# A transformer layer on one core: the sums for the first feed-forward half made beside the values, its first block in seven products, and the values' residual rows added by DVE

## The chip, the cores and the metric

The kernel runs on one core of one Trainium2 chip. A core has a matrix engine (TensorE; the profile calls its matmuls PE and its weight loads PEld), a vector engine (DVE), a scalar engine (ACT), a general engine (POOL) and SyncE (SP), which here only issues transfers (DMA). Each engine works through its own instructions in the order in which they were placed; semaphores tie the engines together. The metric is device microseconds of one execution; lower is better. Before the change the median of 3 runs is 2623.56 us (2621.81 to 2627.48).

## The reference, cut to what matters

One layer of an encoder trunk on 2048 tokens of width 1024, all in 32-bit floats. The change touches the end of step 2 and the beginning of step 3.

```
h = h + rms_norm(y, g_mix_post)                 # after token mixing
u = rms_norm(h, g_x_pre);  m = rms_norm(mem, g_mem)
y = cross_attention(u, m, wq_x, wk_x, wv_x, wo_x)   # 4 heads, 256 memory tokens
h = h + rms_norm(y, g_x_post)
u = rms_norm(h, g_ffn_pre)
y = (silu(u @ w_gate) * (u @ w_up)) @ w_down    # inner width 2816
h = h + rms_norm(y, g_ffn_post)
```

## The kernel before, in words

Every 32-bit matrix is split into a high and a low part of a rounded type ("fp32r"), and a product takes three matmuls (high x high, high x low, low x high; `products`, lines 1009 to 1019). The later phases are written as a list of jobs (`jobs`, line 1277): out projection (mixing), cross-attention scores, cross-attention values, first feed-forward half (tokens 0 to 1023), second half (tokens 1024 to 2047), and the down projection in three passes. In scores and values the weights of the memory side are folded beforehand, so each is one matrix product.

A job multiplies a stationary side, streamed block by block (`streamed`, line 964, whose pieces are called S), with a resident side (called T). Both are cut in 2 x 2 quarters. A block of kind "p" makes the four quarters of its result with eight products of quarters (`eight`); a block of kind "s" makes them with seven (`seven`), for which S and T must also be given as sums and differences of quarters. The T's are numbered by keys: keys 1, 8, 2 and 3 are plain quarters; keys 5, 7, 6 and 4 (`CHAIN`) are differences and sums: 5 is the second column quarter less the first in the upper row, 7 the lower right less the upper right, 6 is 7 plus the upper left, 4 is the lower left less 6. In a block of kind "s" the products come in the order 1, 5, 6, 3, 7, 2, 4; in one of kind "p" two at a time for keys 1, 2, 8, 3. One product has 4 x 3 matmuls of 128x512 where `nk` is 4.

In the mixing, scores and values a block takes 256 tokens (two token tiles of 128) as S, against a weight as T. In the two feed-forward halves it is the other way: u, transposed and stored in `u_d`, is T (1024 tokens of it, quarters by token and by width), and 256 columns of `w_gate` or `w_up` are S. So the first half's T's are made from what the value blocks stored for token tiles 0 to 7 (value blocks 1 to 4 of 8).

`phases` (line 1098) is the planner. It numbers all steps (one product of a block of kind "s", or two of kind "p"), lists each T with the steps that use it, and gives it one of seven T buffers as soon as the last use of what lies there has passed, in the order of first use. A T is loaded in two halves, one per step (two per step in blocks of kind "p"), each into a row tile of 128x1024 (`row_tile`, line 1318; there are nine, shared with everything else of that size, and they are handed out in the order of the program). `resident` (line 893) then splits it with ACT (line 886) and DVE (line 889). For keys 5, 7, 6 and 4 there are two ways: a job with a sums tensor loads them ready-made, one load per half, and splits them two steps later, behind the step's own ACT and DVE work; a job without one (`None`, as the first feed-forward half has) loads the two quarters, keeps those of 7 and 6 for the next key, and adds or subtracts on DVE at line 915. The ready-made sums of the other jobs are computed beside an earlier job (`combined`, line 926, DVE at line 933) and stored.

What follows a block (`after`) is a generator: the planner advances it once per step of the next blocks (twice per step of kind "p"). In `value_block` (line 1440) it takes the mean squares of the two rows y, scales them (line 1459), adds the residual rows h1 by an accumulating transfer that POOL issues (`add`, line 1365), stores h2 through SP, takes mean squares again (line 1336, ACT), scales into two new row tiles u (line 1470), transposes u on PE (line 1252, back through ACT at 1253) and stores it to `u_d`. All other loads and stores are issued by SP (lines 75 and 78), one after another. `mixed_block` (line 1367) does the same for its own residual with plain loads and an addition on DVE (line 1386).

The instructions are traced in this order; a scheduling pass then places them on each engine by their data, their tiles and this order.

Of the kernel before, what the change touches and what calls it, by code (L numbers as in the profile page):

```python
# [11 lines left out]
F32 = mybir.dt.float32  # L12
# [3 lines left out]
ALU = mybir.AluOpType  # L16
AX = mybir.AxisListType

P = 128
# [5 lines left out]
KT = D // P  # L25
NFF = DFF // P
# [22 lines left out]
class Layer:  # L49
# [1011 lines left out]
    def eight(self, S, T, nk, out, addend, halves=False):  # L1061
# [34 lines left out]
        yield  # L1096

    def phases(self, jobs, first, prologue=None):

        steps = [(n, i, p) for n, job in enumerate(jobs) for i, b in enumerate(job[2])
                 for p in self.STEPS[b[0]]]
        takes = [c for job in jobs for b in job[2] for c in self.TAKES[b[0]]]
# [161 lines left out]
    def sums(self, name, src, nk, *tiles):  # L1266
# [7 lines left out]

        return dst, lambda: self.combined(get, nk, dst)

    def jobs(self):
        I = self.I

        def weights(src, r0, nk):  # L1280
            return lambda t, i, j, k0, n: self.load(
                t, src[r0 + (i * nk + k0) * P:r0 + (i * nk + k0 + n) * P, j * 512:(j + 1) * 512]
                .rearrange("(k p) d -> p k d", p=P))

        def ffn_u(b):
            return lambda t, i, j, k0, n: self.load(
                t, self.u_d[4 * i + k0:4 * i + k0 + n, :, b * TB + j * 512:b * TB + (j + 1) * 512]
                .rearrange("k p t -> p k t"))

        def kinds(blocks, n=0):  # L1290
            return [("p" if i < n or i == len(blocks) - 1 else "s",) + b for i, b in enumerate(blocks)]

        def sums(name, src, nk, other=None):
            return self.sums(name, src, nk, self.extra_tile, other or self.gain_tile)

        def in_turn(*what):
            return lambda: itertools.chain.from_iterable(w() for w in what)

        qk, vo = weights(self.qk_d, 0, 4), weights(self.vo_d, 0, 4)
        down = [(weights(I["w_down"], f0 * P, nk), f0, nk) for f0, nk in ((0, 3), (6, 4), (14, 4))]  # L1300
        qk_s, vo_s = sums("qk_s", qk, 4, self.row_tile), sums("vo_s", vo, 4)
        u_s = sums("u_s", ffn_u(1), 4)
        d_s = [sums(f"d_s{c}", src, nk) for c, (src, _, nk) in enumerate(down)]
        jobs = [(self.w_out, 4, kinds([self.mixed_block(n) for n in range(0, NT, 2)], 1), self.out_sums, {1: [qk_s[1]]}),
                (qk, 4, kinds([self.score_block(n) for n in range(0, NT, 2)]), qk_s[0], {1: [vo_s[1]]}),
                (vo, 4, kinds([self.value_block(n) for n in range(0, NT, 2)]), vo_s[0], {})]
        for b in range(NB):
            beside = {2: [in_turn(*(d[1] for d in d_s))]} if b else {4: [u_s[1]]}
            jobs.append((ffn_u(b), 4, kinds([blk for f in range(0, NFF, 2) for blk in self.hidden_blocks(b, f)], 1 - b),
                         u_s[0] if b else None, beside))  # L1310
        for c, (src, f0, nk) in enumerate(down):
            jobs.append((src, nk, kinds([self.down_block(c, f0, nk, n) for n in range(0, NT, 2)]), d_s[c][0], {}))
        k, s, o, f, a = jobs[-1][2][-1]
        jobs[-1][2][-1] = ("s", s, o, f, a)

        return jobs
# [122 lines left out]

    def value_block(self, n):  # L1440
        nc = self.nc
        y, ss = {}, []

        def out(i, j, a, b):
            if not y:
                ss.append(self.small("q_s", 4))
            if i not in y:
                y[i] = self.row_tile()
                if n == 0 and len(y) == 1:
                    self.g_x_post = self.gain(self.I["g_x_post"])  # L1450
                    self.g_ffn_pre = self.extra_tile()
                    self.load(self.g_ffn_pre, self.I["g_ffn_pre"][0:1, :].broadcast_to([P, D]))
            self.squared(y[i][:, j * 512:(j + 1) * 512], a, b, ss[0][:, 2 * i + j:2 * i + j + 1])

        def after():
            r = self.rstds(ss[0])
            s2 = self.small("q_s", 4)
            for i in range(2):
                nc.vector.scalar_tensor_tensor(y[i], y[i], r[:, i:i + 1], self.g_x_post, ALU.mult, ALU.mult)
                self.add(y[i], self.h1_d, n + i)  # L1460
                self.store(self.h2_d[(n + i) * P:(n + i + 1) * P, :], y[i])
                yield
            yield
            for i in range(2):
                self.mean_squares(y[i], i, s2)
                yield
            r = self.rstds(s2)
            u = [self.row_tile() for _ in range(2)]
            for i in range(2):
                nc.vector.scalar_tensor_tensor(u[i], y[i], r[:, i:i + 1], self.g_ffn_pre, ALU.mult, ALU.mult)  # L1470
                yield
            yield
            for i in range(2):
                self.store_transposed(self.u_d, n + i, self.transposed(u[i], u[i]))
                yield

        return self.tokens(self.pt_d, n), out, after, None

    def hidden_blocks(self, b, f):
# [130 lines left out]
```

## Time and profile before

| what | us |
|---|---|
| median of 3 runs | 2623.56 (2621.81 to 2627.48) |
| the profiled execution, whole | 2629.38 |
| its span in the profile | 2627.7 |
| PE busy | 2560.7 (97%) |
| DVE busy | 1732.1 (66%) |
| ACT busy | 1262.0 (48%) |
| POOL busy | 431.3 (16%) |
| mean granted clock of PE | 0.993 |

The profile is of one execution. Times in it count from the start of the span; an engine's idle time carries the name of what released it. Matmuls overlap, so the mean length of one is longer than the distance between two. A tile's buffer number is left out of its name: "row" is any of the nine row tiles, "sraw" a streamed block, "part" a copied partial result, "psm" a PSUM bank of the products, "pss" one of the transposes; "h_d" stands for h1 and h2.

### The profile page before, as it was taken

How to read it: one execution, taken by the hardware profiler on the slowest of the kernel's cores; microseconds unless marked ns; L12 is line 12 of the kernel's file. 1: busy time of each engine (PE TensorE's matmuls, PEld its weight loads, DVE VectorE, ACT ScalarE, POOL GpSimd, SP SyncE). 2: the span in 40 equal slices, each digit the busy share in tenths (PEclk: the TensorE clock that was granted, in tenths of full speed). 3: DMA queues.
4: the chain of work that ended last, by engine and by line, in shares of the span. 5: the costliest groups of instructions: out<-in, count | busy, mean ns of one | idle time of the engine just before them, and what ended most of it. 6: DMA issues, size and time to landing. Idle time of an engine off the chain costs nothing.

```text
span 2627.7 us, 34806 instructions
## 1 busy us (share of the span) xinstructions
PE 2560.7 (97%) x12329; PEld 2142.2 (82%) x12329; DVE 1732.1 (66%) x2725; ACT 1262.0 (48%) x2628; POOL 431.3 (16%) x627
## 2 busy tenths in 40 slices
PE   7999999999999999999989999999999999999998
PEld 6877888878988887888878888888888888888886
DVE  7675478877545778777676655566666556564656
ACT  5463366655545566565563333344333334453543
POOL 4231344331311332213310000000000000000022
PEclk9999999999999999999999999999999999999999
DMA  5445655675877886666884632353566434576888
GB/s 184 127 149 174 187 158 159 197 232 158 239 256 261 306 279 235 216 233 176 242 276 131 196 101 82 102 191 123 168 203 197 155 121 172 183 215 177 268 209 216
DMA packets 354158, 502.87 MB, mean 191 GB/s; under 512 B 20672, under 2 KB 237760, under 8 KB 353984
## 3 DMA queue, kind: packets, MB, share of 16 engines
q1 hardware_dynamic: 345632, 470.24, 55.0%
q0 software_dynamic: 8352, 30.41, 6.6%
q8 instruction: 97, 1.59, 0.3%
q14 instruction: 77, 0.63, 0.1%
HBM read 338.05 MB, written 162.53 MB: 191 GB/s over the span
## 4 chain that ended last, share of the span: by engine, by line
PE 81%; DMA 8%; DVE 4%; ACT 3%; issue 2%; POOL 1%; SPq 1%; DVEq 0%; POOLq 0%; ACTq 0%
PE psm L1017 23%; PE psm L1018 23%; PE psm L1019 23%; PE psg L158 2%; PE psg L157 2%; PE psg L156 2%; PE pss L1252 1%; DMA qd<-z_d 1%; DMA z<-in_w_out_dram 1%; DMA u_d<-row 1%; DMA qq<-z_d 1%; SPq L75 1%; DVE wlo L889 0%; DMA h_d<-row 0%; DMA row<-y_d 0%
## 5 line engine op out<-in xcount | busy, mean ns | idle before, releaser
L1017 PE MATMUL psm<-T,S 128*128 128x512 f32 x2699 | 1046.6, 392 | 18.7 <-ACT part L1032 9.4
L1018 PE MATMUL psm<-T,S 128*128 128x512 f32 x2699 | 1052.6, 391 | 0.7 <-DVE T L889 0.6
L1019 PE MATMUL psm<-T,S 128*128 128x512 f32 x2699 | 1042.7, 391 | 2.0 <-DVE S L889 2.0
L1017 PEld LDWEIGHTS psm<-T,S 128*128 128x128 f32 x2699 | 508.2, 188 | 129.7 <-ACT part L1032 10.6
L1019 PEld LDWEIGHTS psm<-T,S 128*128 128x128 f32 x2699 | 508.2, 188 | 108.3 <-DVE S L889 2.9
L1018 PEld LDWEIGHTS psm<-T,S 128*128 128x128 f32 x2699 | 508.3, 188 | 106.1 <-DVE T L889 2.1
L889 DVE TENSOR_TENSOR S<-sraw,S 128x512 fp32r<-128x512 f32 (+1 forms) x320 | 218.4, 689 | 215.9 <-ACT S L886 198.6
L886 ACT ACTIVATE S<-sum 128x512 fp32r<-128x512 f32 (+1 forms) x310 | 186.5, 620 | 345.0 <-PE psm L1019 257.9
L889 DVE TENSOR_TENSOR S<-sum,S 128x512 fp32r<-128x512 f32 (+1 forms) x368 | 246.8, 681 | 58.0 <-ACT S L886 34.6
L1032 ACT ACTIVATE part<-psm 128x512 f32<-128x512 f32 x270 | 159.9, 596 | 244.8 <-PE psm L1019 229.3
L886 ACT ACTIVATE S<-sraw 128x512 fp32r<-128x512 f32 (+1 forms) x273 | 168.0, 616 | 120.9 <-PE psm L1019 104.7
L1365 POOL DMA_DIRECT2D row<-y_d x28 | 25.8, 921 | 1124.4 <-DVE row L1541 1032.7
L889 DVE TENSOR_TENSOR T<-row,T 128x1024 fp32r<-128x1024 f32 (+1 forms) x122 | 143.7, 1191 | 66.5 <-ACT T L886 66.0
L156 PE MATMUL psg<-u,whi 128*128 128x512 f32 x352 | 141.5, 402 | 1.6 <-POOL whi L888 1.6
L158 PE MATMUL psg<-u,wlo 128*128 128x512 f32 x352 | 140.2, 398 | 0.9 <-DVE wlo L889 0.9
L157 PE MATMUL psg<-u,whi 128*128 128x512 f32 x352 | 140.3, 398 | 0.0
L886 ACT ACTIVATE T<-row 128x1024 fp32r<-128x1024 f32 x122 | 122.1, 1027 | 23.9 <-DVE row L915 7.8
L1336 ACT ACTIVATE junk<-row 128x512 f32<-128x512 f32 x160 | 99.9, 625 | 67.6 <-DVE row L1358 26.8
L888 POOL TENSOR_SCALAR S<-sum 128x512 fp32r<-128x512 f32 x58 | 48.3, 832 | 288.4 <-PE psm L1019 228.9
L1492 DVE TENSOR_TENSOR row<-psm,part 128x512 f32<-128x512 f32 x63 | 41.7, 688 | 59.5 <-PE psm L1019 59.4
L1501 DVE TENSOR_TENSOR part<-psm,part 128x512 f32<-128x512 f32 x60 | 39.8, 688 | 61.1 <-PE psm L1019 60.9
L156 PEld LDWEIGHTS psg<-u,whi 128*128 128x128 f32 x352 | 66.7, 189 | 14.7 <-POOL whi L888 2.1
(335 smaller groups left out, 3634.0 us busy)
## 6 DMA issues: line engine op xcount, KB each, us to landing
sraw<-in_w_gate_dram SPq DMA_DIRECT2D x44, 512.0 KB, 3.9
sraw<-in_w_up_dram SPq DMA_DIRECT2D x44, 512.0 KB, 4.0
hid_d<-row SPq DMA_DIRECT2D x44, 512.0 KB, 2.6
h_d<-row SPq DMA_DIRECT2D x32, 512.0 KB, 5.8
y_d<-row SPq DMA_DIRECT2D x32, 512.0 KB, 3.2
sraw<-hid_d SPq DMA_DIRECT2D x32, 512.0 KB, 5.1
row<-h_d POOLq DMA_DIRECT2D x30, 512.0 KB, 6.8
row<-u_d SPq DMA_DIRECT2D x30, 512.0 KB, 6.1
```

The lines of the kernel that those rows point to most:

```text
L156: nc.tensor.matmul(ps, ah, bh, start=(i == 0), stop=False)
L157: nc.tensor.matmul(ps, ah, bl, start=False, stop=False)
L158: nc.tensor.matmul(ps, al, bh, start=False, stop=(i == n - 1))
L886: self.nc.scalar.activation(hi, raw, AF.Copy)
L888: self.nc.gpsimd.tensor_scalar(hi, raw, 1.0, 1.0, ALU.mult, ALU.mult)
L889: self.nc.vector.tensor_tensor(lo, raw, f32(hi), ALU.subtract)
L1017: nc.tensor.matmul(ps, s[:, 0, k, :], t[:, 0, k, :], start=st, stop=False, **kw)
L1018: nc.tensor.matmul(ps, s[:, 0, k, :], t[:, 1, k, :], start=False, stop=False, **kw)
L1019: nc.tensor.matmul(ps, s[:, 1, k, :], t[:, 0, k, :], start=False, stop=sp, **kw)
L1032: nc.scalar.activation(t, ps, AF.Copy)
L1336: self.nc.scalar.activation(junk, a, AF.Square, scale=float(D) ** -0.5, accum_out=to)
L1492: nc.vector.tensor_tensor(d, a, c, ALU.add)
```

## The change

- `jobs`: a tensor `u0_s` holds ready-made sums for the first feed-forward half, and that job loads them (it had `None`). Its first block is of kind "s" (seven products) where it was "p" (eight). Its last block stays "p".
- `token_sums`: in the value blocks for token tiles 4 to 7, after u has been transposed and stored, the transposed u of token tile n - 4 is loaded back from `u_d` into a row tile o; eight half-row operations on DVE per block (four per token tile) turn u and o, in place, into the four sums for those 128 tokens, and four stores per token tile write them to `u0_s`.
- `value_block`: the residual rows x are loaded by SP into two row tiles when the block's first output is made, and DVE adds them; the accumulating transfers go. u overwrites y instead of taking new row tiles. The order of the `yield`s moves: there is one step less between the h2 stores and the mean squares, the step between the second scaling's factor and the scaling is new, and the one between the scaling and the transposes goes, so that the transposes are queued one step earlier.

```diff
+    def token_sums(self, a, o, n):
+        nc = self.nc
+        nc.vector.tensor_tensor(a[:, 4:8], a[:, 4:8], a[:, 0:4], ALU.subtract)
+        nc.vector.tensor_tensor(a[:, 0:4], a[:, 0:4], o[:, 0:4], ALU.subtract)
+        yield
+        nc.vector.tensor_tensor(o[:, 0:4], o[:, 0:4], a[:, 4:8], ALU.add)
+        nc.vector.tensor_tensor(o[:, 4:8], o[:, 4:8], o[:, 0:4], ALU.subtract)
+        for c, t in enumerate((a[:, 0:4], a[:, 4:8], o[:, 0:4], o[:, 4:8])):
+            self.store(self.u0_s[c].rearrange("p (k t) -> p k t", k=4)[:, :, n * P:(n + 1) * P], t)
+        yield
...
+        self.u0_s = self.tc.dram_tile([4, P, 4 * 512], F32, name="u0_s")
...
-            jobs.append((ffn_u(b), 4, kinds([blk for f in range(0, NFF, 2) for blk in self.hidden_blocks(b, f)], 1 - b),
-                         u_s[0] if b else None, beside))
+            jobs.append((ffn_u(b), 4, kinds([blk for f in range(0, NFF, 2) for blk in self.hidden_blocks(b, f)]),
+                         u_s[0] if b else self.u0_s, beside))
...
     def value_block(self, n):
-        y, ss = {}, []
+        y, x, ss, u, o = {}, [], [], {}, {}
         def out(i, j, a, b):
             if not y:
+                x.extend(self.rows_of(self.h1_d, n + r) for r in range(2))
...
             for i in range(2):
                 nc.vector.scalar_tensor_tensor(y[i], y[i], r[:, i:i + 1], self.g_x_post, ALU.mult, ALU.mult)
-                self.add(y[i], self.h1_d, n + i)
+                nc.vector.tensor_tensor(y[i], y[i], x[i], ALU.add)
                 self.store(self.h2_d[(n + i) * P:(n + i + 1) * P, :], y[i])
                 yield
-            yield
             for i in range(2):
                 self.mean_squares(y[i], i, s2)
                 yield
             r = self.rstds(s2)
-            u = [self.row_tile() for _ in range(2)]
-            for i in range(2):
-                nc.vector.scalar_tensor_tensor(u[i], y[i], r[:, i:i + 1], self.g_ffn_pre, ALU.mult, ALU.mult)
-                yield
             yield
             for i in range(2):
-                self.store_transposed(self.u_d, n + i, self.transposed(u[i], u[i]))
+                nc.vector.scalar_tensor_tensor(y[i], y[i], r[:, i:i + 1], self.g_ffn_pre, ALU.mult, ALU.mult)
                 yield
+            for i in range(2):
+                u[i] = self.transposed(y[i], y[i])
+                self.store_transposed(self.u_d, n + i, u[i])
+                if 4 <= n < 8:
+                    o[i] = self.row_tile().rearrange("p (k t) -> p k t", k=KT)
+                    self.load(o[i], self.u_d[:, :, (n - 4 + i) * P:(n - 3 + i) * P].rearrange("k p t -> p k t"))
+                yield
+            if o:
+                yield
+                for i in range(2):
+                    yield from self.token_sums(u[i], o[i], n - 4 + i)
```

## The prediction

> **What bounds the kernel now.** First the page: its busy times, then its chain.
>
> ```profile
> span 2627.7 us, 34806 instructions
> PE 2560.7 (97%) x12329; PEld 2142.2 (82%) x12329; DVE 1732.1 (66%) x2725; ACT 1262.0 (48%) x2628; POOL 431.3 (16%) x627
> PE 81%; DMA 8%; DVE 4%; ACT 3%; issue 2%; POOL 1%; SPq 1%; DVEq 0%; POOLq 0%; ACTq 0%
> ```
>
> PE holds the end, so only two things can shorten the run: fewer matmuls, or fewer holes between them. Second, the busy times by stretch around the edit (columns: stretch, its length, busy time and count of PE, PEld, DVE, ACT, POOL, granted clock, DMA share, GB/s).
>
> ```profile
> 1200.00:1250.00 50.00, 50.00 (x242) 41.83 (x241) 34.42 (x44) 28.90 (x68) 18.34 (x30) 1.00 0.72 197
> 1250.00:1300.00 50.00, 50.00 (x243) 41.70 (x242) 31.70 (x39) 27.43 (x63) 17.32 (x27) 1.00 0.85 222
> 1300.00:1350.00 50.00, 48.62 (x231) 40.34 (x230) 32.23 (x33) 30.19 (x60) 10.42 (x18) 1.00 0.99 295
> ...
> 1355.00:1375.00 20.00, 14.20 (x44) 9.79 (x43) 15.37 (x18) 12.18 (x19) 0.94 (x2) 0.74 0.80 288
> ...
> 2200.00:2300.00 100.00, 100.00 (x443) 82.80 (x442) 56.55 (x98) 40.99 (x78) 0.00 (x0) 1.00 0.49 169
> ```
>
> The value blocks (about 1165 to 1331) keep PE full. The first feed-forward blocks, just after them, do not. The undisturbed row gives a matmul every 100/443 = 0.226 us; 20 us would hold 88.6, and 1355 to 1375 holds 44, so 44.6 x 0.226 = 10.1 us are lost: 20 - 14.20 = 5.8 idle, 4.3 at a lower clock. With the 1.4 us wait just before 1350 (the fourth row of the next view) that is 11.5 us. Third, who PE waits for: in 1350 to 1400 (three rows), before it (one), and from 1400 to the end (two).
>
> ```profile
> PE psm L1017 <- ACT T L886: 4.4, 2, 4.1
> PE psm L1017 <- ACT row L1494: 0.8, 1, 0.8
> PE psm L1018 <- DVE T L889: 0.6, 1, 0.6
> ...
> PE pss L1252 <- DVE row L1470: 1.4, 1, 1.4
> ...
> PE psm L1017 <- DVE row L1541: 2.2, 2, 1.3
> PE psm L1017 <- ACT row L1545: 0.7, 1, 0.7
> ```
>
> So the hole is a T (a resident operand) made too late. After 1400 PE waits only in the down projection (L1541, L1545): the second half's first block, whose sums are loaded ready-made, shows no wait at all. Fourth, why that T is late: the chain from 1300 to 1400, then SP's own waits from 1195 to 1400.
>
> ```profile
> 1330.09 7.51 DMA u_d<-row
> ...
> 1343.01 11.90 DMA u_d<-row
> 1354.97 5.99 DMA row<-u_d
> ```
> ```profile
> SPq L78 <- DMA row<-h_d: 54.4, 16, 8.6
> ...
> SPq L75 <- DVE row L1470: 9.8, 4, 5.8
> ...
> SPq L75 <- DMA u_d<-row: 3.6, 2, 2.3
> ```
>
> A store of u (11.90) had to land before a row tile came free for a load of T (5.99). SP, one in-order queue, also stood 54.4 us behind the 16 accumulating loads, because each h2 store waits for one.
>
> **The change, part by part.** Rows for the prices (the first three are groups of instructions by shape; then one line's instructions; then DMA issues with us to landing; then two queues in 1195 to 1360):
>
> ```profile
> L1386 DVE TENSOR_TENSOR row<-row,row 128x1024 f32<-128x1024 f32 x16 | 19.8, 1269 | 0.0
> ...
> L915 DVE TENSOR_TENSOR row<-row,row 128x1024 f32<-128x1024 f32 x8 | 9.8, 1223 | 1.0 <-DMA row<-u_d 0.8
> ...
> L889 DVE TENSOR_TENSOR T<-row,T 128x1024 fp32r<-128x1024 f32 x114 | 138.5, 1226 | 62.8 <-ACT T L886 62.3
> ...
> L992 DVE TENSOR_TENSOR sum<-sraw,sraw x92: 548/685/1105, 60.0 to 2584.1; 128x512 f32<-128x512 f32 x85, 128x384 f32<-128x384 f32 x7
> ...
> row<-h_d POOLq DMA_DIRECT2D x30, 512.0 KB, 6.8
> ...
> row<-in_x_dram SPq DMA_DIRECT2D x16, 512.0 KB, 6.9
> ...
> u_d<-row SPq DMA_DIRECT2D x16, 512.0 KB, 5.0
> ...
> y_d<-ys SPq DMA_DIRECT2D x16, 256.0 KB, 3.3
> ...
> q1 hardware_dynamic: 26091, 32.03, 58.1%
> q0 software_dynamic: 2261, 8.21, 28.8%
> ```
>
> *Seven products for eight.* One product is 4 x 3 = 12 matmuls: 12 x 0.226 = 2.7 us off PE, on the path. The block gains 3 S splits and 4 sums on DVE (7 x 0.69 = 4.8 us) and 3 adds at its outputs (2.1). The second key-8 operand goes: two loads, two T splits (2 x 1.23).
>
> *Ready sums.* Of 20 loads for the first half's T's (2 each for keys 1, 2, 8, 3; 4, 4, 2, 2 for 7, 5, 6, 4), 14 stay: 6 from u_d, 8 from u0_s. The 8 adds of L915 (9.8 us) leave exactly the stretch where PE starves. In exchange the deadline comes nearer: key 5 was wanted a whole 22 us block (8 x 2.7) and one product after the boundary, now only one product after it. What covers that: u0_s is complete about two value blocks earlier. The planner starts key 5 two steps before the last value block, and each T half needs one row tile where keys 7 and 5 took two. Counted by the planner's rule, the peak demand on the nine row tiles was 13 (in the last value block: 2 u of the block two back, 2 y and 1 u of the one before, 2 y of its own, 2 of key 3, 4 of key 7); it becomes 12 (2 y of the block before, 2 x and 2 y of its own, 2 each of keys 3, 7 and 2). So the crush remains, shorter. What is late next is the last operands, keys 2 and 4: their tiles are freed only by the stores of u for tokens 12 and 13 and by the last x tiles.
>
> The remaining hole is bounded below by nothing (the second half's first block, no wait) and above by all 11.5 us. The nearest row with the same crowd of row tiles is the start of the scores, whose PE waits from 800 to 1180 are:
>
> ```profile
> PE psm L1017 <- ACT part L1032: 4.3, 3, 2.5
> PE psm L1019 <- DVE S L889: 2.0, 1, 2.0
> PE psm L1017 <- ACT T L886: 0.5, 1, 0.5
> ```
>
> That boundary has ready sums and crowded tiles; I take 3.5 us.
>
> *Residual rows by DVE.* 16 POOL issues and accumulating transfers go; 16 plain loads come on SP, early, from a source complete since the mixing. DVE gets 16 x 1.27 = 20 us, 2.5 per value block. From the scaling to the h2 store a row waits 1.3 us in place of an issue and 6.8 us. By the two queues, a software MB costs 28.8/8.21 = 3.5% of the engines there, a hardware MB 1.8%: moving 8.2 MB frees 14%, the 6.3 MB of new stores and loads take 11%, six T loads less give 6% back. So transfers cost nothing net. u now overwrites y, so its scaling waits until the h2 store has landed (h_d<-row, queued earlier now); some five steps (about 14 us) lie between, and behind that wait on DVE stand the S splits for PE. I cost it at nothing, at most one landing like u_d's 5.0.
>
> *The token sums* are 16 adds of 128x512 (16 x 0.69 = 11 us), 16 stores of 256 KB (3.3 each) and 4 loads, in value blocks 5 and 6 of 8. Here the cover is thin, by the load of DVE in one value block:
>
> ```profile
> 1229.00:1249.85 20.85, 14.26 (x18) 1.00 0.79 203
> ```
>
> 14.3 + 2.5 = 16.8 us of 20.85; with eight sums 22.3, that is 1.5 us too many in each of the two blocks. The first add of each token tile waits for the u store it overwrites (5.0), so DVE may also stand. And row tiles run out: two u, two o, the next block's two y, then two x and one y make nine when the second y of the following block wants a tenth; it must wait for sums to be stored. The same squeeze exists before, in the mixing (DVE in order of time; then two stretches there and one of the scores):
>
> ```profile
> 903.81 0.69 DVE L1358 TENSOR_TENSOR row<-psm,part 128x512 f32<-128x512 f32 x1 [3.21 <-DMA h1t_d<-row]
> ```
> ```profile
> 900.00:920.00 20.00, 20.00 (x98) 16.70 (x97) 14.19 (x17) 10.86 (x28) 4.86 (x10) 1.00 0.85 280
> 920.00:940.00 20.00, 17.96 (x85) 14.66 (x84) 14.98 (x19) 10.53 (x28) 5.99 (x9) 1.00 0.89 295
> ...
> 1020.00:1040.00 20.00, 20.00 (x98) 16.61 (x97) 18.34 (x37) 12.62 (x33) 5.41 (x8) 1.00 0.49 158
> ```
>
> DVE stood 3.2 us for a row tile around 903 and PE, full from 900 to 920, did not notice; with DVE 92% busy from 1020 PE was full too. The cost is between nothing and 2 x (1.5 + 5.0) = 13; nearest to these rows I take 1 us a block, 2 in all.
>
> **Sum** against the profiled run (2629.38 us): -2.7 (product) - 11.5 (old hole) + 3.5 (what stays of it) + 2 (value blocks) = -8.7, so 2620.7. The profiled run stands 5.8 above the median of the three runs, 2623.56; from that the forecast is 2615.
>
> *A rule of the Trainium skill, weighed.* Row first:
>
> ```profile
> 1360.49 0.80 PE L1017 MATMUL psm<-T,S 128*128 128x512 f32 x1 [4.13 <-ACT T L886]
> ```
>
> After this single wait of 4.13 us the clock is 0.74 over 1355 to 1375. The Trainium skill, "TensorE: Matmul & The Clock Gate", "What's actually happening", says that one idle window of about 3.4 us drops the array to half clock, and that it takes about as long of busy work to come back. The trace agrees: 4.3 us lost beside 5.8 idle. By that rule a remaining hole of 3.5 us in one piece costs an estimated 1.7 us more, and the sum would be 2617; in pieces, as in the scores' rows, it stays 2615.
>
> **The rivals.** *B, no change: the hole moves.* The deadline comes 22 us nearer, and row tiles, not loads, are the limit (9.8 and 3.6 us of SP's waits are for them). If keys 6, 7, 2 and 4 come late one after another, all 11.5 us stay: -2.7 + 2 = -0.7; with 4 us recovered -4.7. Time about 2621. Against it: the loads for T fall from 20 to 14, and stores of u no longer queue behind accumulating loads.
>
> *C, slower: the tenth row tile.* In value blocks 5 and 6 DVE stands at an output until a sum's store lands, with S splits behind it. If the wait is a store of u (5.0) and one of a sum (3.3), less one product of slack (2.7), PE stops 5.6 us, and at the old hole's ratio (4.3 to 5.8) the low clock adds 4.1: 9.7 a block, 19 for two. Against the gains of 2.7 + 8 = 10.7 this is +9: 2632. It decides from about 5 us a block. For it: 22.3 us of DVE in 20.85. Against it: 903, above.
>
> **How the numbers follow.** Forecast 0.53, B 0.19, C 0.21, smaller stalls elsewhere that eat all of it (the x tiles crowd the first value blocks too) 0.07. About 0.2%, 5.2 us, is what a measurement can tell. B falls mostly within it: 0.16, the rest faster. C and the last are slower but for a bit: faster 0.56, same 0.18, slower 0.26. The best case is -2.7 - 11.5 = 2609, and 1 for the spread makes 2608; upward 2630 leaves out the worse half of C. The forecast's own range is 2608 to 2618.
>
> **What would show it.** The stretch 1355 to 1375 (some 20 us earlier now) should hold 75 or more matmuls per 20 us; PE's x12329 falls by about 12; L915's row group and L1365's 16 h_d issues are gone; SP's waits on row<-h_d shrink by some 54 us; DVE in value blocks 5 and 6 is near 100%, PE full. I am wrong if PE shows waits of 2 us or more between 1250 and 1330, on DVE's S or on ACT's part, or if the new first block waits on T from key 7 on.

## The result, and the profile after

The changed kernel is slower, a little: 2634.42 us median of 7 runs (2629.95 to 2637.78) beside 2627.48 (2621.81 to 2632.98) for the kernel before in the same session. The ratio is 1.0025, 95% interval 1.0013 to 1.0037, so +6.6 us. The forecast was -8.7 us; on its base, 2623.56, the ratio makes 2630.1. The page of the profiled execution after (2630.55 us as a whole):

```profile
span 2628.8 us, 34838 instructions
PE 2559.4 (97%) x12317; PEld 2139.5 (81%) x12317; DVE 1753.4 (67%) x2757; ACT 1261.6 (48%) x2632; POOL 426.2 (16%) x611
```

PE has 12 instructions fewer, as forecast. The two spans nearly agree only because the part ahead of the values, which the change does not touch, went some 3 us faster in this execution. So the touched part is cut out: from the last store of the scores (pt_d) to the first of the feed-forward (hid_d), and from there to the last store of hid_d. Columns are stretch, length, busy time and count of PE, PEld, DVE, ACT, POOL, granted clock, DMA share, GB/s. First before, then after:

```profile
1173.40:1388.00 214.60, 207.39 (x955) 169.99 (x954) 150.60 (x179) 124.22 (x260) 52.22 (x84) 0.98 0.80 228
1388.00:2191.30 803.30, 803.30 (x3546) 665.38 (x3545) 486.22 (x712) 302.54 (x517) 0.00 (x0) 1.00 0.46 150
```
```profile
1169.90:1386.80 216.90, 204.13 (x928) 165.21 (x927) 172.75 (x212) 123.43 (x261) 48.01 (x68) 0.97 0.74 239
1386.80:2193.50 806.70, 806.70 (x3561) 667.98 (x3560) 485.43 (x712) 302.88 (x519) 0.00 (x0) 1.00 0.46 150
```

The second stretch is full in both. (The first store lies at another place of PE's work, 15 instructions earlier, so only the sum of the two can be compared.) Together: 1017.9 us and 4501 PE instructions before, 1023.6 and 4489 after, +5.7 us, which agrees with the ratio's +6.6. Idle time of PE goes from 214.60 - 207.39 = 7.2 to 216.90 - 204.13 = 12.8, +5.6; 12 instructions fewer at 0.226 make -2.7; the rest, 5.7 - 5.6 + 2.7 = +2.8, is matmuls farther apart. About half of it is the clock: PE was busy for 7.6 us at half clock before and for 10.6 after (rows in the last section), so 3.8 and 5.3 us were lost, +1.5. The other 1.3 stays open. In the same view, where the loss lies, first before, then after:

```profile
1250.00:1310.00 60.00, 60.00 (x287) 49.98 (x286) 37.44 (x45) 33.84 (x79) 19.27 (x31) 1.00 0.88 241
1310.00:1380.00 70.00, 62.82 (x277) 50.20 (x276) 49.38 (x53) 42.70 (x76) 9.61 (x16) 0.93 0.91 281
```
```profile
1250.00:1310.00 60.00, 56.85 (x266) 46.23 (x265) 54.14 (x69) 32.44 (x75) 20.98 (x24) 1.00 0.98 317
1310.00:1380.00 70.00, 60.41 (x262) 47.47 (x261) 47.39 (x54) 44.08 (x83) 6.90 (x12) 0.90 0.65 212
```

The boundary, 1310 to 1380, has 9.6 us of idle time in place of 7.2: the old hole was not closed, it grew. And value blocks 5 and 6, full before, have a new 3.2 us in 1250 to 1310, with DVE busy for 54.14 of 60. Whom PE waits for, after, from 1150 to 1310 (two rows) and from 1310 to 1400 (three):

```profile
PE pss L1252 <- DVE row L1483: 2.2, 2, 1.7
PE psm L1019 <- DVE S L889: 1.0, 1, 1.0
...
PE psm L1017 <- ACT T L886: 4.8, 2, 3.3
PE psm L1018 <- DVE T L889: 3.9, 4, 2.0
PE pss L1252 <- DVE row L1483: 1.0, 1, 1.0
```

At the boundary it is T again, late on ACT and then on DVE. Why ACT was late is in the time lines of SP, ACT and PE (start, length, instruction, and in brackets what ended the idle time ahead of it; "u_s" stands for u0_s too):

```profile
1310.11 7.75 SPq L75 DMA_DIRECT2D row<-u_s  x3
...
1323.89 0.32 SPq L75 DMA_DIRECT2D row<-h_d  x1
...
1324.75 0.42 SPq L78 DMA_DIRECT2D u_d<-row  x1
1325.22 1.69 SPq L75 DMA_DIRECT2D row<-h_d  x1
...
1332.10 1.09 ACT L1373 ACTIVATE row<-psm 128x512 f32<-128x512 f32 x2 [4.49 <-DMA u_d<-row]
...
1335.43 1.05 ACT L886 ACTIVATE T<-row 128x1024 fp32r<-128x1024 f32 x1
...
1336.53 0.50 PE L1017 MATMUL psm<-T,S 128*128 128x512 f32 x1 [3.27 <-ACT T L886]
```

The last value block loads its residual rows (row<-h_d, 1323.89 and 1325.22) when its first output is made, and the two row tiles for them are handed out just ahead of those that the outputs themselves are copied into. ACT makes these copies (L1373), and one of them has to wait for a tile to come free, which a store of u frees. The chain of waits has that store as its longest piece at this place:

```profile
1324.75 7.33 DMA u_d<-row
```

ACT works in order. It stood 4.49 us, then ran from 1332.10 without a break through its backlog, among it the T split at 1335.43, and PE got its T at 1336.53. Loads and splits come in the order of first use, so the T's can be told apart by counting: this one is the second half of key 5, whose load SP had issued by 1317.9 (the x3 row). So the load came in time and the split did not. The second part of the hole is key 7, and there the load itself was late:

```profile
1349.26 0.95 SPq L75 DMA_DIRECT2D row<-u_s  x1
...
1353.46 0.50 PE L1018 MATMUL psm<-T,S 128*128 128x512 f32 x1 [2.03 <-DVE T L889]
...
1355.34 1.06 ACT L886 ACTIVATE T<-row 128x1024 fp32r<-128x1024 f32 x1 [3.25 <-DMA row<-u_s]
...
1356.45 0.80 PE L1017 MATMUL psm<-T,S 128*128 128x512 f32 x1 [1.48 <-ACT T L886]
```

Of the 8.7 us of waits for T (4.8 + 3.9), key 5 has about 4.0, key 7 about 4.0 and key 3 the rest; keys 2 and 4 have none. What the change promised inside the machinery did happen: SP no longer waits for row<-h_d in 1195 to 1400 (54.4 us before), the additions of L915 for this half are gone.

### The profile page after: what moved, and what is told of

Read it like the earlier page. It is cut to its first block, busy times and chain, and to the rows that moved or that the text cites. A ratio compares the mean times of both kernels' runs of the same rounds, so it can differ in the third digit from the quotient of the medians.

```text
span 2628.8 us, 34838 instructions
## 1 busy us (share of the span) xinstructions
PE 2559.4 (97%) x12317; PEld 2139.5 (81%) x12317; DVE 1753.4 (67%) x2757; ACT 1261.6 (48%) x2632; POOL 426.2 (16%) x611
## 4 chain that ended last, share of the span: by engine, by line
PE 81%; DMA 8%; DVE 5%; ACT 3%; issue 2%; POOL 1%; SPq 1%; DVEq 0%; POOLq 0%; ACTq 0%
PE psm L1017 23%; PE psm L1018 23%; PE psm L1019 23%; PE psg L158 2%; PE psg L157 2%; PE psg L156 2%; PE pss L1252 1%; DMA z<-in_w_out_dram 1%; DMA qd<-z_d 1%; SPq L75 1%; ACT T L886 1%; DMA row<-qk_d 1%; DVE T L889 0%; DMA z_d<-z 0%; DMA row<-d_s 0%
```

## The experiments

Three theories were set against each other. The expectations call them N, R and D. N: the seven products bring the deadline of the T's nearer, and that costs more than the product. R: the order in which row tiles are handed out, with the residual rows ahead of the outputs, makes ACT stand. D: the token sums, by their work on DVE and their row tiles in value blocks 5 and 6, make PE wait there. For each run the two stretches of the section above were added up; the table has them beside the measured ratio. The sums are of one execution each and the ratios of several, so that the two can differ by 2 or 3 us (e5, e12). A diff is against the changed kernel where nothing else is said.

| kernel | both stretches, us | PE instr. | PE idle, us | ratio to before (95%) |
|---|---|---|---|---|
| before | 1017.9 | 4501 | 7.2 | 1 |
| after | 1023.6 | 4489 | 12.8 | 1.0025 (1.0013 to 1.0037) |
| e1_residual_only | 1022.0 | 4501 | 10.1 | 1.0017 (1.0005 to 1.0028) |
| e2_sums_only | 1021.9 | 4489 | 11.4 | 1.0008 (0.9997 to 1.0019) |
| e3_eight_products | 1015.5 | 4501 | 6.3 | 0.9988 (0.9977 to 0.9998) |
| e4_pool_last_two | 1011.7 | 4489 | 5.4 | 0.9978 (0.9969 to 0.9987) |
| e5_x_in_after | 1016.3 | 4489 | 6.8 | 0.9983 (0.9974 to 0.9993) |
| e6_pool_last_two_step | 1011.5 | 4488 | 4.9 | 0.9975 (0.9965 to 0.9985) |
| e7_pool_last_two_no_sums | 1008.9 | 4490 | 3.1 | 0.9964 (0.9950 to 0.9977) |
| e8_seven_only | 1029.3 | 4490 | 15.8 | 1.0047 (1.0030 to 1.0063) |
| e9_pool_last_two_eight | 1011.6 | 4502 | 4.5 | 0.9974 (0.9964 to 0.9984) |
| e10_pool_all | 1027.1 | 4489 | 15.1 | 1.0041 (1.0028 to 1.0055) |
| e11_pool_from_6 | 1015.9 | 4488 | 8.3 | 0.9995 (0.9985 to 1.0005) |
| e12_pool_last_one | 1016.5 | 4488 | 9.0 | 0.9987 (0.9973 to 1.0002) |

**The parts alone.** e1 keeps the new `value_block` and drops the sums and the seven products; e2 does the reverse; e8, against the kernel before, has the seven products alone, with sums made on the fly; e3 is the whole change but for the seven products.

```diff
# e1_residual_only (and no token_sums in value_block)
-    jobs.append((ffn_u(b), 4, kinds([...]), u_s[0] if b else self.u0_s, beside))
+    jobs.append((ffn_u(b), 4, kinds([...], 1 - b), u_s[0] if b else None, beside))
# e2_sums_only (and u in row tiles of its own, the steps as before)
-    x.extend(self.rows_of(self.h1_d, n + r) for r in range(2))
...
-    nc.vector.tensor_tensor(y[i], y[i], x[i], ALU.add)
+    self.add(y[i], self.h1_d, n + i)
# e8_seven_only, against the kernel before
-    jobs.append((ffn_u(b), 4, kinds([...], 1 - b), u_s[0] if b else None, beside))
+    jobs.append((ffn_u(b), 4, kinds([...]), u_s[0] if b else None, beside))
# e3_eight_products
-    jobs.append((ffn_u(b), 4, kinds([...]), u_s[0] if b else self.u0_s, beside))
+    jobs.append((ffn_u(b), 4, kinds([...], 1 - b), u_s[0] if b else self.u0_s, beside))
```

> Only the value blocks' new residual rows (plain loads into two more row tiles, addition on DVE, u in place of y, the moved steps); the first feed-forward half keeps its sums on the fly and eight products in its first block. Changed kernel against before: +6.9 us by the medians; its profile shows the scalar engine standing 4.5 us in the last value block for a row tile and PE losing 3.1 us in value blocks 5 and 6. Theory R (row tiles: the two x tiles of the last value block take the tiles that its outputs and the T loads want): slower than before by 3 to 8 us, with the wait of ACT on u_d in the last value block. Theory D (DVE and row tiles of the token sums in value blocks 5 and 6): no sums here, so within 3 us of before. Theory N (the seven products bring the deadline of the T's too near): within 3 us of before, or faster.

> Only the token sums and the seven products; the residual comes by the accumulating transfers and u takes row tiles of its own, as before the change. R: faster than before by 3 to 8 us (2.7 of the product and part of the old hole). D: slower than before by 0 to 4 us, PE losing 3 us or more between 1250 and 1300. N: slower, the hole at the start of the feed-forward half as large as in the changed kernel (about 10 us idle between 1320 and 1360).

> The kernel before, with seven products in the first block of the first feed-forward half and nothing else changed (its sums still made on the fly from double loads). N (a deadline nearer by a block uncovers the late T's): 4 to 12 us slower than before, the hole at 1335 to 1360 twice as large. Otherwise 2.7 us faster than before.

> The changed kernel with eight products in the first block of the first feed-forward half, the ready sums kept. R: the hole stays, 0 to 3 us slower than the changed kernel or equal to it. N: the sums get a whole block of cover, the hole closes but for 3 us: faster than the changed kernel by 3 to 6 us, level with before. D: slower than the changed kernel by 2.7 us.

Nearly all that PE waits for in e8 from 1310 to 1400 is T, two rows of it (0.8 us more is for a scaling):

```profile
PE psm L1017 <- ACT T L886: 10.3, 3, 5.8
PE psm L1018 <- DVE T L889: 4.6, 4, 2.0
```

Seven products without anything else cost 12 us (1.0047), though they take 12 matmuls away: N holds by itself. By the ratios e3, with eight, is some 10 us faster than the changed kernel, where N forecast 3 to 6 and R nothing. In it ACT still stands at its outputs for u's store, but PE is full where after it was not (ACT's waits in 1150 to 1400, then a stretch):

```profile
ACT row L1373 <- DMA u_d<-row: 3.4, 1, 3.4
```
```profile
1330.00:1345.00 15.00, 15.00 (x72) 12.49 (x71) 10.13 (x10) 11.32 (x23) 4.05 (x6) 1.00 0.60 206
```

So much the same stand of ACT (3.4 us in place of 4.5) costs PE nothing when the T is wanted a block later. e1 came out as R forecast, 4.5 us slower by the ratio and with ACT standing for a tile. The sums are not there to be loaded in it, so DVE makes them at L915, where it stood 2.97 us for a load of u, and the scaling of u came behind that (PE's largest wait in 1310 to 1400, then ACT's on the tile):

```profile
PE pss L1252 <- DVE row L1482: 6.4, 1, 6.4
```
```profile
ACT row L1372 <- DMA u_d<-row: 3.5, 1, 3.5
```

e2 has no x tiles at all, and R would have it 3 to 8 us faster than before; it is 1.0008. N's hole of about 10 us between 1320 and 1360 is 4.0. D fits: 0 to 4 us slower (2.1 by the ratio, whose interval includes no change), with 3 us or more lost between 1250 and 1300. The stretch beside the sums, then ACT's and DVE's waits for a store of u (1150 to 1400):

```profile
1250.00:1310.00 60.00, 53.45 (x243) 43.70 (x242) 43.17 (x59) 27.21 (x63) 20.09 (x26) 0.94 1.01 275
```
```profile
ACT row L1373 <- DMA u_d<-row: 8.0, 1, 8.0
...
DVE row L1280 <- DMA u_d<-row: 10.4, 4, 5.4
```

L1280 is the first subtraction of `token_sums`. It writes over u in place, so it has to wait until u's store has landed: 10.4 us in e2, 0.4 in the changed kernel. All four waits lie between 1250 and 1310, where PE lost 60 - 53.45 = 6.5 of the 11.4 us that it stood idle. In that stretch SP stood 12.3 us behind accumulating transfers, ahead of its stores, which fits; no run shows that link by itself. The boundary, without x tiles, lost 4.9 us (1310 to 1380) in place of 9.6, although ACT stood 8.0 us there for a tile. So R has its part there, but with u in tiles of its own ACT can stand as well. D alone is not the whole either: in e3 above and e4 below the sums stay, and the time falls.

**Freeing the tiles at the boundary.** e4 lets the last two value blocks add their residual by POOL's accumulating transfer again, so that they take no x tiles; e12 only the last one (`n < 14`). e5 keeps the additions on DVE everywhere, but takes the x tiles after the block's outputs instead of ahead of them.

```diff
# e4_pool_last_two (e12: n < 14)
-    x.extend(self.rows_of(self.h1_d, n + r) for r in range(2))
+    if n < 12:
+        x.extend(self.rows_of(self.h1_d, n + r) for r in range(2))
...
-    nc.vector.tensor_tensor(y[i], y[i], x[i], ALU.add)
+    if x:
+        nc.vector.tensor_tensor(y[i], y[i], x[i], ALU.add)
+    else:
+        self.add(y[i], self.h1_d, n + i)
# e5_x_in_after: in `out`, and then at the start of `after`
-    x.extend(self.rows_of(self.h1_d, n + r) for r in range(2))
...
+    x = [self.rows_of(self.h1_d, n + r) for r in range(2)]
```

> The changed kernel with the accumulating transfers back in the last two value blocks alone, so that no x tile is held at the boundary. R: faster than the changed kernel by 4 to 9 us, the wait of ACT for a row tile in the last value block gone, level with before or faster by up to 3 us. D and N: as the changed kernel within 2 us.

> The changed kernel with the residual rows' loads moved by three steps: they are asked for (and take their two row tiles) where the block's follow-up begins, after the block's own outputs have their tiles, instead of at its first output. The addition stays on DVE, the loads on SP, the sums and the seven products stay. R (the x tiles, taken ahead of the outputs, are what ACT waits for): ACT's wait for a row tile in the last value block shrinks to 2 us or less, 5 to 13 us faster than the changed kernel, like the run with POOL in the last two blocks. If it was instead SP's extra loads or DVE's additions: as the changed kernel within 2 us.

> The changed kernel with the accumulating transfer back in the last value block alone. R, in its narrow form (the two x tiles of the very last block are the ones that ACT's outputs and the T loads miss): as the run with POOL in the last two blocks, 0.9978 within 0.0012. If the block before it shares the fault: between that run and the changed kernel, 0.999 to 1.001.

e5 moves the two loads of each block and nothing else, and goes from 1.0025 to 0.9983: ACT stands 2.2 us in place of 4.5 (R said 2 or less), PE's wait for ACT's T from 1310 to 1400 shrinks from 4.8 us to 0.5, and its idle time from 1310 to 1380 from 9.6 to 4.2. R holds. e4 goes further, 0.9978; its two stretches, then PE's waits from 1310 to 1400:

```profile
1162.40:1367.30 204.90, 199.46 (x928) 162.11 (x927) 167.46 (x208) 122.99 (x261) 52.33 (x72) 1.00 0.80 249
1367.30:2174.10 806.80, 806.80 (x3561) 668.27 (x3561) 485.47 (x711) 303.02 (x519) 0.00 (x0) 1.00 0.45 150
```
```profile
PE psm L1018 <- DVE T L889: 1.5, 3, 0.8
PE psm L1017 <- ACT part L1032: 0.8, 1, 0.8
```

The hole is 2.3 us, and the clock stays at 1.00. Against the changed kernel both stretches lose 11.9 us, 7.3 of it idle time. e12 gets 7.1 of the 11.9 us (1016.5): its ACT still stands 2.4 us for a u store and 2.7 for another row tile, as if the last block but one shared the fault. The times do not decide it: 0.9987 lies within what the narrow form of R forecast (0.9978 within 0.0012), and its interval reaches across the other forecast (0.999 to 1.001).

**The value blocks.** e6 is e4 with one more `yield` between the scaling of u and its transposes, which would help if the moved step were what makes PE wait for the scaling. e7 is e4 without the sixteen additions and subtractions of `token_sums`: it stores raw rows in their place, so its first half is computed from wrong sums.

```diff
# e6_pool_last_two_step
                 nc.vector.scalar_tensor_tensor(y[i], y[i], r[:, i:i + 1], self.g_ffn_pre, ALU.mult, ALU.mult)
                 yield
+            yield
# e7_pool_last_two_no_sums
-        nc.vector.tensor_tensor(a[:, 4:8], a[:, 4:8], a[:, 0:4], ALU.subtract)
-        nc.vector.tensor_tensor(a[:, 0:4], a[:, 0:4], o[:, 0:4], ALU.subtract)
...
-        nc.vector.tensor_tensor(o[:, 0:4], o[:, 0:4], a[:, 4:8], ALU.add)
-        nc.vector.tensor_tensor(o[:, 4:8], o[:, 4:8], o[:, 0:4], ALU.subtract)
```

> The run with POOL in the last two value blocks, with one more step between u's scaling and its transposes, as there was before the change. If PE's waits of 2.0 us for the scaled rows in value blocks 5 and 6 come from the transposes being queued a step early: they go, 2 to 3 us faster than that run. If they come from DVE being full of sums: they move to S or stay, same within 1.5 us.

> The run with POOL in the last two value blocks, with the sixteen additions and subtractions of the token sums left out (the raw rows are stored in their place, all loads and stores kept), so the first feed-forward half is computed from wrong sums. D (DVE's load in value blocks 5 and 6 costs PE): the waits of about 3 us between 1250 and 1310 go, 3 us faster than that run. If transfers or the queue order cost them: same within 1 us.

e6 is e4 again, with the same 2.0 us of waits for the scaling: the step is not it. In e7 the value blocks get most of their time back; e4 first, then e7:

```profile
1250.00:1310.00 60.00, 56.89 (x268) 46.32 (x267) 52.02 (x64) 34.29 (x79) 20.30 (x27) 1.00 0.96 309
```
```profile
1250.00:1310.00 60.00, 58.77 (x278) 48.33 (x277) 46.26 (x53) 35.17 (x80) 15.76 (x27) 1.00 0.95 304
```

Idle time falls from 3.1 to 1.2 us with DVE's load; 1.9 of the 3.1 go with the sums, their work and the waits on it. What makes the other 1.2 was not taken apart.

**Where POOL should add.** e10 is the changed kernel with POOL adding in all value blocks (`if False` in place of `n < 12`), e11 from the fourth block on (`n < 6`).

> The changed kernel with the accumulating transfers in all value blocks; u in place of y, the moved steps, the token sums and the seven products stay. It differs from the run of sums alone (1.0008) by u in place of y and the moved steps only. R: u's own two row tiles were what made that run's scalar engine wait 8.0 us for a row tile and its DVE 10.4 us; in place they go, 3 to 7 us faster than that run, 0.997 to 0.999 of before. If the accumulating transfers were what held it up: as that run within 2 us.

> The changed kernel with the accumulating transfers from token tile 6 on, so that the blocks beside the token sums have neither x tiles nor the two additions of 2.5 us on DVE. D: the waits of about 3 us in value blocks 5 and 6 shrink to 1 us or less and it is 1 to 3 us faster than the run with POOL in the last two blocks. If row tiles or transfers bind there: same as that run within 1.5 us.

Both missed: e10 is 1.0041, slower than e2 and not faster, and e11 is 0.9995 beside e4's 0.9978. In both the mean squares on ACT, and after them everything up to the transposes, stand behind the accumulating transfers. ACT's and then PE's waits in e10 from 1150 to 1330, and ACT's in e11 from 1150 to 1400:

```profile
ACT junk L1349 <- DMA row<-h_d: 22.4, 9, 6.5
...
PE pss L1252 <- DVE row L1487: 5.3, 3, 2.7
PE psm L1019 <- DVE S L889: 3.3, 2, 2.0
```
```profile
ACT junk L1349 <- DMA row<-h_d: 14.4, 6, 7.0
```

In the same stretch, 1150 to 1330, this wait is 3.2 us in the kernel before and 0.8 in e2, which have the same transfers. e10 differs from e2 in two things, u in place of y and the moved steps. The mean squares read y in both. But one step less lies between the addition and the mean squares in e10: two steps of 2.7 us make 5.4, three make 8.1, and a transfer took 7.6 to land (e10, median from 1240 to 1310). That speaks for the moved step as the cause of ACT's waits. u in place shows itself too: its scaling on DVE waits 4.4 us for stores of h2 (L1487 on h_d<-row, 1150 to 1400). No run takes the two apart.

DVE stands at L1280 here too, for u's store: 7.7 us in e10 and 6.5 in e11 from 1250 to 1310, beside 0.5 in e4. So e11 has 6.5 us less of work on DVE there than e4 (45.5 us busy, 52.0 in e4), and PE still idles 3.6 us, where it idles 3.1 in e4.

Between e10 and e4 lie 15.4 us in the stretches and 0.63% in the ratios: with u in place and the steps as the change has them, adding the residual on DVE is worth about 16 us in the first six blocks. In the last two it costs, by the order of the tiles: with the x tiles taken later (e5), DVE adds there too, and the ratio is e4's within the intervals.

**The product, where tiles are free.** e9 is e4 with eight products.

```diff
-    jobs.append((ffn_u(b), 4, kinds([...]), u_s[0] if b else self.u0_s, beside))
+    jobs.append((ffn_u(b), 4, kinds([...], 1 - b), u_s[0] if b else self.u0_s, beside))
```

> The run with POOL in the last two value blocks, with eight products in the first block of the first feed-forward half. With the row tiles freed, the late T's should no longer be uncovered by the seventh product: 1 to 3 us slower than that run, for the product's 2.7 us. If seven products cost in themselves, as in the changed kernel (where eight gained some 10 us): faster than that run.

It is not slower than e4 as far as the ratios can tell (0.9974 and 0.9978, each within 0.0010, which is 2.6 us). In its stretches 13 more instructions (12 in the program; a record more is missing in e4) take the same time:

```profile
1166.30:1371.40 205.10, 200.60 (x942) 164.90 (x941) 164.09 (x200) 122.13 (x258) 51.38 (x72) 1.00 0.82 260
1371.40:2177.90 806.50, 806.50 (x3560) 667.81 (x3559) 485.77 (x711) 303.43 (x519) 0.00 (x0) 1.00 0.45 149
```

0.9 us of the missing 2.9 (13 x 0.226) is idle time that e4 has more, mostly its waits for T (e9 waits only 1.5 us from 1310 to 1400, for a scaling). The other 2 us lie inside what is counted as busy, 199.46 us for 928 instructions against 200.60 for 942. What stretches them is open; the clock is 1.00 in all four rows.

## Why the prediction was wrong, by its own steps

- **"12 x 0.226 = 2.7 us off PE, on the path": right in count, not on the path.** PE did lose 12 instructions. But alone they cost 12 us (e8), and with the tiles freed they bring nothing that e4 and e9 can show.
- **"What stays of it, 3.5": this step failed.** I took the start of the scores as the nearest row, and it was not near. The idle time at the boundary went from 7.2 to 9.6 us, and half clock cost 5.3 us in place of 3.8, so -8.0 was wrong by some 12 us: this place lost 2.4 + 1.5 = 3.9 us where I expected to gain 8.0. Two things were behind it, and with the sums ready-made it took both. The nearer deadline I had named, but let the ready sums pay for it ("what covers that"): key 5's rows were indeed asked for in time, and its second half was split too late all the same. The other I had counted, but not followed: "the peak demand was 13, it becomes 12" says how many want a tile, not in what order they get one. The two x tiles are handed out ahead of the block's own output, ACT is the engine that stands, and the T splits queue behind it on ACT. Undoing only the order (e5) or only the seven products (e3) brings 7 to 8 us each in the stretches. "What is late next is the last operands, keys 2 and 4" was wrong too: PE waited for keys 5 and 7, about 4 us each, and for 2 and 4 not at all.
- **"I take 1 us a block, 2 in all": undersized.** 3.2 us of idle time were measured. My row from the scores (DVE 92% busy, PE full) did not carry over: with DVE at 90% over 60 us PE did wait, for the scaling ahead of the transposes and for an S split. Of the signs that I named for being wrong, a wait on DVE's S in 1250 to 1330 is there at 1.0 us, under my bound; the larger wait in that place is one that I had not named, on L1483. The last sign, waits for T "from key 7 on", came true with key 7's 4.0 us. The first sign failed: the 20 us from 1335 to 1355 hold 52 instructions of PE, 16 of them transposes, and not 75 matmuls. "I cost it at nothing" of the scaling in place was about right in itself: it waits for no h2 store in the lists; it waits for its turn on DVE.
- **"Transfers cost nothing net": right.** From 1195 to 1360 the two queues took 58.1 + 28.8 = 86.9% of the DMA engines before, and the one that is left took 80.5% after. The 54.4 us of SP's waits on row<-h_d are gone. And the additions on DVE are worth more than I put on them, which was nothing: with the steps as the change has them, e10 without them is 15.4 us slower than e4.
- **The rivals.** B (the hole moves) had the mechanism, T after T late from tiles, but bounded its harm at no change. C had the sign and the tile, but the wrong place and engine: DVE's wait for a sum's load (1.5 us, L1281 on row<-u_d, in 1150 to 1400) stopped nobody long; it was ACT, in the last value block. That its 2632 is near the 2630.1 is luck. "Smaller stalls elsewhere (the x tiles crowd ...)" named the x tiles, in the first value blocks and with a chance of 0.07; they crowded the last.
- **The clock.** I let a remaining hole "in pieces" cost no clock, and one in a single piece 1.7 us. Both were too little. After the change a hole in pieces of at most 3.3 us cost 5.3 us of clock, and the old hole had cost 3.8 (I put it at 4.3, and called a rule that gives 1.7 confirmed by it): the low stretches lasted 6.8 to 10.2 us (last section).

With tiles freed, e4 gets two thirds of what I forecast for the change itself, -0.22% against -0.33%. e4, e6 and e9, which differ by less than their intervals, are the fastest whole kernels here and beat both the kernel before and the changed one.

## What to carry to other kernels

When prefetched rows share a pool of tiles with outputs, count not only how many tiles are wanted at the peak but in which order they are handed out, and which in-order engine makes the copy that comes last in that order: everything queued behind it is late too. A saved matmul product brings nothing if it moves the next operand's deadline nearer than that operand can be made; try the deadline alone (e8) and the tile order alone (e5) before both. And a change that is slower as a whole can hold a faster kernel: here it was enough to leave the last two blocks out of one part.

## What the runs showed of the hardware

Short waits lower the granted clock, and not always. In e5 a single wait of 1.80 us (PE in order of time) was followed by a stretch at 0.75:

```profile
1333.27 0.50 PE L1017 MATMUL psm<-T,S 128*128 128x512 f32 x1 [1.80 <-ACT part L1032]
```
```profile
1335.00:1340.00 5.00, 5.00 (x21) 4.01 (x20) 3.81 (x4) 5.00 (x9) 1.40 (x3) 0.75 0.68 217
```

In e12 a wait of 2.01 us at the same place was followed by full clock:

```profile
1334.71 0.50 PE L1017 MATMUL psm<-T,S 128*128 128x512 f32 x1 [2.01 <-ACT part L1032]
```
```profile
1335.00:1340.00 5.00, 5.00 (x27) 4.12 (x26) 3.81 (x5) 5.00 (x9) 2.93 (x4) 1.00 0.61 199
```

After the change, the 3.27 us wait and the shorter ones behind it gave 0.56 in 1340 to 1345 and 0.50 in 1355 to 1360. How long the clock stays low, before (one stretch) and after (two):

```profile
1359.24:1369.48 10.24, 7.61 (x16) 5.26 (x17) 8.08 (x10) 6.87 (x10) 0.00 (x0) 0.50 0.86 305
```
```profile
1337.59:1344.42 6.83, 5.67 (x17) 4.41 (x18) 5.88 (x7) 6.83 (x15) 3.96 (x6) 0.50 0.48 154
1354.65:1361.48 6.83, 4.89 (x12) 3.03 (x11) 3.33 (x4) 6.11 (x10) 0.00 (x0) 0.50 1.00 339
```

In e5 it was 3.41 us, from 1334.12 to 1337.53. So the price came in steps of 3.41 us at half clock here: one after that wait in e5, two and two after the change, three before it. The Trainium skill, "TensorE: Matmul & The Clock Gate", "What's actually happening", puts the drop after an idle window of about 3.4 us, and says that this window runs freely. e5 differs from the first figure, since 1.80 us was enough; that the outcome hangs on where a wait falls in a free-running window would fit e5 beside e12, and the lengths fit such a window, but where one begins no run here shows.

The other surprise is the price of accumulating transfers in a chain: 22.4 us of ACT's waits in e10, up to 6.5 us for one, where the same transfers in the kernel before, with u in tiles of its own and the mean squares one step later, left PE full.
